# Projections of an attention layer: the two halves of each q, k and gate part in one PSUM bank, wide evacuations, and another split of the last scaling

## The chip, the core and the metric

The kernel runs on one core of a Trainium2 chip. The metric is the device time of one execution in microseconds (us). The engines are named as in the profile: PE is TensorE (PEld its weight loads), DVE is VectorE, ACT is ScalarE, POOL is GpSimd, SP is SyncE, whose queue issues nearly all DMAs.

## The reference

One layer of block attention on 256 positions of width 1024, 16 heads of 64, everything in float32:

```python
h = rms_norm(x, norm_g)
q, k, v, gate = jnp.split(h @ w_in, 4, axis=-1)     # w_in is 1024 x 4096
o = moba_attention(to_heads(q), to_heads(k), to_heads(v))
x = x + (o * jax.nn.silu(gate)) @ w_out             # w_out is 1024 x 1024
return rms_norm(x, final_norm_g)
```

With 256 positions there is a single block, so the attention is a plain causal softmax with a linear position penalty per head.

## The kernel before

*Precision.* A float32 matrix a is split into a rounded high part ah (written by ACT) and a remainder al = a - ah (written by DVE); a product is three matmuls, ah bh + al bh + ah bl. The input x times the norm's gain is held transposed as xh and xl, and each piece of weights w as whi and wlo, 128x1024 elements, one ACT and one DVE instruction per piece, from a piece that SP's queue fetched. The 1/rms of a position is not applied to x but to the results.

*Projections.* PARTS lists the order: v (first 512 columns), then q, k, g of 256 columns each, and so on, 14 parts. The first v part runs while the data arrive. A q, k or g part has 256 output columns, that is two pairs of heads, f = 0 and 1, of 128 rows each. Its loop (L661 to L684) takes two banks by take_now, one for each f, and runs over 8 slices of the depth, in each over f and the three terms, with 256 columns (positions) per matmul.

*Evacuation.* After the last matmul of each f, evac starts a fiber fiber_evac (L484 to L526): DVE multiplies the bank by rows (1/rms of each position, repeated in all partitions) or rows8 (the same over 8) into z, 128x256; ACT writes the high part of z as q or k (or tanh(z/2) for the gate, into sg, whose tile is called head in the profile), and DVE the remainder (L519) or (tanh + 1) z (L525). fiber_norm makes rows and rows8 on ACT (L650, L651). Since the gate is not halved, the softmax sums are doubled (L399) before the reciprocal.

*Attention.* scores(p) multiplies q and k of the two pairs p and p + 1 in four banks (L353, 16 or 20 matmuls shown per block); it waits for both pairs' q and k. Then each pair has its own fiber_pair: masks and minima on DVE (L386, L389), exponentials on ACT, scaling by the reciprocals (pr, L412), transposes on PE (L111), their split (pth on ACT, ptl on DVE), the product with v (matmuls pth, ptl with vv), the sum of its halves (cs on ACT, og on DVE, L467), the gate product (L471), and its split into oh (ACT) and ol (DVE, L476).

*What sets the order.* The program is written out by a planner at build time. Class Plan keeps one clock per engine, with costs per instruction. Fibers yield the time from which they want to go on; side, called after each matmul, advances the first fiber that is ready by that clock, and fill places the splits of the next weight piece when they become due. So a changed cost or a changed number of fibers moves instructions of other stages too. Each engine then runs its list in order and waits where an operand is not there. A tile pool with n buffers lets n tiles live at once; q had 4 tiles of one pair, k had 3.

*Output.* The output projection adds, for each of 8 pairs k, three matmuls per group of columns, with 512, 512 columns for the first 128 positions (block 0, m = 0) and 512, 256, 256 for the second (block 1, m = 1). Its tail (L712 to L749) adds x (L731), squares and sums on ACT (L737, the sum of a row comes by a separate accumulator read) or, for a block's last group, on DVE (L733), multiplies by the final gain (L738, L743), adds up the mean square (L739), takes the power -1/2 on POOL (L742), scales (ACT L744 for the first 512 columns, DVE L747 for the rest) and stores by SP's queue (L749). The scaled block lies in a tile that is called bias in the profile.

Of the kernel before, what the change touches and what calls it, by code (L numbers as in the profile page):

```python
# [13 lines left out]
P = 128  # L14
# [27 lines left out]
for seg in LAID:  # L42
# [2 lines left out]
        WIDTH[seg] = (NK if seg[1] == 0 else 0) + S * (seg[2] - seg[1])  # L45
    else:
        WIDTH[seg] = D if seg[0] == "t" else KP * GW // seg[3]
NKB = 3
NPR = 3
NPT = 3  # L50
SLACK = 1000.0
# [36 lines left out]
def trunk(ctx: ExitStack, tc, laid, fin_g, out):  # L88
# [6 lines left out]
    sm = ctx.enter_context(tc.tile_pool(name="sm", bufs=8))  # L95
    sp = ctx.enter_context(tc.tile_pool(name="sp", bufs=NPR))
    ptp = ctx.enter_context(tc.tile_pool(name="ptp", bufs=NPT))
    qp = ctx.enter_context(tc.tile_pool(name="qp", bufs=4))
    khp = ctx.enter_context(tc.tile_pool(name="khp", bufs=NKB))
    zp = ctx.enter_context(tc.tile_pool(name="zp", bufs=3))  # L100
    csp = ctx.enter_context(tc.tile_pool(name="csp", bufs=2))
    ogp = ctx.enter_context(tc.tile_pool(name="ogp", bufs=2))
    psum = ctx.enter_context(tc.tile_pool(name="psum", bufs=1, space=bass.MemoryType.PSUM))


    def mm(o, a, b, start, stop, n, dep=0.0):
        nc.tensor.matmul(o, a, b, start=start, stop=stop)  # L107
        return plan.mm(n, dep)

    def tr(o, a, dep=0.0):  # L110
# [103 lines left out]
    rstd = [const.tile([P, 1], F32, name=f"rstd{m}") for m in range(NM)]  # L214
    rows = const.tile([P, S], F32, name="rows")
    rows8 = const.tile([P, S], F32, name="rows8")

    def make_bias(h):
        slope = -(2.0 ** (-8.0 * (h + 1) / H))
# [104 lines left out]
    def scores(p):  # L324


        while not all(u in at_k and u in at_q for u in (p, p + 1)):
            yield poll()
        yield max(t[u] for t in (at_k, at_q) for u in (p, p + 1))
        while stage["s"] < p:  # L330
            yield poll()
        while True:
            b0 = take(keep[0] + 3)
            if b0 is not None:
                break
            yield poll()
        both = [b0] + [take_now() for _ in range(3)]
        plan.pe += SWITCH
        for u in (p, p + 1):
            of_pair[u] = both[2 * (u - p):2 * (u - p) + 2], {}  # L340
        for m, c in ((1, slice(0, S)), (0, slice(S, S + P))):
            for u in (p, p + 1):
                bs, at_s = of_pair[u]
                (qh, ql), kt = qs[u], ks[u]
# [12 lines left out]
        stage["s"] = p + 2  # L357
        yield 0

    def fiber_pair(p):  # L360
# [35 lines left out]
                    give(bs[a], d)  # L396
        stage["e"] += 1
        yield e - 400
        nc.vector.tensor_scalar(rs, rs, 2.0, None, op0=ALU.mult)  # L399
        dve(4, e)  # L400
        yield plan.t["dve"] - 50
        nc.vector.reciprocal(ri, rs)
        d = d_ri = dve(4, e, extra=157)
        for a in range(2):
# [74 lines left out]
    def evac(kind, j, f, b, r):  # L479
        fibers.insert(0, [0.0, fiber_evac(kind, j, f, b, r)])  # L480
        if kind == "k":
            fibers.append([0.0, fiber_pair(2 * j + f)])

    def fiber_evac(kind, j, f, b, r):  # L484
        ps = b["t"][:, :S]
        p = 2 * j + f
        if kind == "v":
            ps = b["t"]
# [13 lines left out]
        while not have_rows:  # L502
            yield poll()
        yield max(r, have_rows[0]) - 200
        z = zp.tile([P, S], F32, name="z")
        nc.vector.tensor_mul(z, ps, rows8 if kind == "q" else rows)  # L506
        d = dve(S, max(r, have_rows[0]))
        give(b, d)
        if kind == "k":
            while stage["s"] <= p - NKB:  # L510
                yield poll()
        yield d - 100
        if kind != "g":
            pool = qp if kind == "q" else khp
            both = pool.tile([P, 2, S], F32R, name=kind)
            hi, lo = both[:, 0], both[:, 1]
            e = act(hi, z, AF.Copy, S, d, False)
            yield e - 100
            nc.vector.tensor_sub(lo, z, f32(hi))  # L519
            (qs if kind == "q" else ks)[p] = (hi, lo) if kind == "q" else both  # L520
            (at_q if kind == "q" else at_k)[p] = dve(S, e)
        else:
            e = act(sg[:, p, :], z, AF.Tanh, S, d, False, scale=0.5)
            yield e - 100
            nc.vector.scalar_tensor_tensor(sg[:, p, :], sg[:, p, :], 1.0, z, op0=ALU.add, op1=ALU.mult)  # L525
            at_g[p] = dve(S, e)  # L526

    with tc.manual_schedule():

# [96 lines left out]
        def fiber_norm():  # L626
# [22 lines left out]
            yield r - 200  # L649
            act(rows, b["t"][:, :S], AF.Copy, S, r, True)  # L650
            d = act(rows8, b["t"][:, :S], AF.Copy, S, r, True, scale=DH ** -0.5)  # L651
            give(b, d)
            have_rows.append(d)
# [5 lines left out]

        i = 3  # L660
        for kind, j in PARTS[1:]:  # L661
            acc = [take_now() for _ in range(2)]
            dep = [b["free"] for b in acc]
            w = CW if kind == "v" else GW
            kp = KP * GW // w
            for k in range(NK):
# [5 lines left out]
                for f in range(2):  # L672
                    fs = slice(f * P, (f + 1) * P)
                    for jj, (xx, ww) in enumerate(((xh, whi), (xl, whi), (xh, wlo))):
                        if kind == "v":
                            o, a, b = acc[f]["t"], xx[k][:, fs], ww[i][:, kk * w:(kk + 1) * w]
                        else:
                            o, a, b = acc[f]["t"][:, :S], ww[i][:, kk * w + f * P:kk * w + (f + 1) * P], xx[k]
                        r = mm(o, a, b, k == 0 and jj == 0, k == NK - 1 and jj == 2, w if kind == "v" else S,
                               max(wr, dep[f]))  # L680
                        fill()
                        side()
                    if k == NK - 1:
                        evac(kind, j, f, acc[f], r)  # L684


# [16 lines left out]
        for k in range(NK):  # L703
            use(N_IN + k - (k >= 5))
            if k < NK - 4:
                until(lambda: k in at_o)
                plan.pe = max(plan.pe, at_o[k])
                for m in range(NM):
                    for c0, c1 in GROUPS[m]:
                        outmm(k, m, c0, c1, accs[m, c0]["t"][:, :c1 - c0])  # L710
        use(N_PIECES)
        for m in range(NM):  # L712
            y, z, sq = xs[m], spare[:, m * D:(m + 1) * D], spare[:, 2 * D + m * CW:2 * D + (m + 1) * CW]
            ns = len(GROUPS[m])
# [9 lines left out]
            for u, (c0, c1) in enumerate(GROUPS[m]):  # L724
                c = slice(c0, c1)
                o = accs[m, c0]["t"][:, :c1 - c0]
                for k in range(late, NK):
                    until(lambda: k in at_o)
                    plan.pe = max(plan.pe, at_o[k])
                    outmm(k, m, c0, c1, o)  # L730
                nc.vector.tensor_add(y[:, c], o, y[:, c])  # L731
                if u == ns - 1:
                    nc.vector.tensor_tensor_reduce(sq[:, :c1 - c0], y[:, c], y[:, c], scale=1.0 / D,  # L733
                                                   scalar=ms[:, u - 1:u], op0=ALU.mult, op1=ALU.add,
                                                   accum_out=ms[:, u:u + 1])
# [53 lines left out]
```

## Time and profile before

| | |
|---|---|
| three runs | 145.71, 146.01, 146.97 us, median 146.01 |
| profiled execution | 146.19 us, its span in the trace 144.4 us |
| PE busy | 136.7 us (95%), weight loads 125.9 us |
| DVE busy | 123.0 us (85%) |
| ACT busy | 93.3 us (65%) |
| POOL busy | 13.7 us (10%) |
| TensorE clock granted | 0.993 of full speed over the span |

The span reaches from the first to the last instruction; the rest of the execution's own time lies around it. Busy times of different engines overlap. A matmul's busy time is modelled and longer than the distance to the next start, since matmuls are pipelined. In rows with a time in front, the first number is the start in us from the span's start, the second the duration, and what stands in brackets is idle time of that engine just before and what ended it.

### The profile page before, as it was taken

The page shows a single profiled execution, that of the slowest core. Times are in us where ns is not written, and L with a number is a line of the kernel's source. Part 1 is how long each engine was busy: PE and PEld are TensorE (multiplying, and loading weights), DVE is VectorE, ACT ScalarE, POOL GpSimd, SP SyncE. Part 2 cuts the span into 40 slices and gives each one's busy share as a digit, 9 for nine tenths or more (in the row PEclk, how much of TensorE's full clock was granted, in tenths as well). Part 3 has the DMA queues.
Part 4 walks back from the last instruction along what each step waited for, and adds up shares of the span by engine and source line. Part 5 has one row for each costly group of instructions (what it writes and reads, how often), then busy time and mean ns, then how long its engine had stood idle before and what let it go on. Part 6 is the DMA issues. An engine that isn't in the chain of part 4 may idle for free.

```text
span 144.4 us, 2750 instructions
## 1 busy us (share of the span) xinstructions
PE 136.7 (95%) x993; PEld 125.9 (87%) x993; DVE 123.0 (85%) x306; ACT 93.3 (65%) x198; POOL 13.7 (10%) x29
## 2 busy tenths in 40 slices
PE   7999999999999999999999999999999999999910
PEld 5678899999999999999987899999999889887900
DVE  0999489979988899989999998978989989965870
ACT  3498979665789572979855798536394884622331
POOL 7892140000000000000000000000000000000210
PEclk9999999999999999999999999999999999999997
DMA  5999998588005275622456601567756040000123
GB/s 167 327 394 413 408 390 301 204 284 292 31 0 183 112 242 178 211 100 86 174 176 199 235 9 32 178 210 231 246 168 222 33 138 9 0 0 0 41 109 145
DMA packets 8078, 24.83 MB, mean 172 GB/s; under 512 B 896, under 2 KB 1408, under 8 KB 8064
## 3 DMA queue, kind: packets, MB, share of 16 engines
q1 hardware_dynamic: 7632, 23.73, 47.5%
q10 hardware_dynamic: 432, 0.92, 1.7%
q8 instruction: 8, 0.13, 0.4%
q14 instruction: 6, 0.05, 0.1%
HBM read 23.60 MB, written 1.05 MB: 171 GB/s over the span
## 4 chain that ended last, share of the span: by engine, by line
PE 77%; DMA 8%; DVE 4%; issue 4%; ACT 2%; SPq 1%; POOL 1%; POOLq 0%; ACTq 0%
PE bank L107 70%; DMA w<-in_laid 8%; PE bank L111 4%; PE bank L353 4%; DVE wlo L251 2%; ACT whi L118 1%; DVE x L731 1%; SPq L157 1%; POOL fr L742 1%; DVE bias L733 1%; ACT bias L737 1%; ACT bias L744 0%; POOLq L785 0%; DVE xl L572 0%; ACT head L118 0%
## 5 line engine op out<-in xcount | busy, mean ns | idle before, releaser
L107 PE MATMUL bank<-xh,wlo 128*128 128x256 f32 x192 | 55.3, 288 | 0.0
L107 PE MATMUL bank<-xh,whi 128*128 128x256 f32 x192 | 55.1, 287 | 0.0
L107 PE MATMUL bank<-xl,whi 128*128 128x256 f32 x192 | 55.1, 287 | 0.0
L118 ACT ACTIVATE whi<-w 128x1024 fp32r<-128x1024 f32 (+1 forms) x43 | 42.0, 977 | 17.8 <-PE bank L107 10.4
L251 DVE TENSOR_TENSOR wlo<-w,whi 128x1024 fp32r<-128x1024 f32 (+1 forms) x43 | 48.6, 1139 | 4.6 <-ACT whi L118 4.5
L107 PEld LDWEIGHTS bank<-xh,wlo 128*128 128x128 f32 x192 | 36.2, 189 | 0.3 <-DVE wlo L251 0.2
L107 PEld LDWEIGHTS bank<-xh,whi 128*128 128x128 f32 x192 | 36.2, 189 | 0.2
L107 PEld LDWEIGHTS bank<-xl,whi 128*128 128x128 f32 x192 | 36.3, 189 | 0.1
L118 ACT ACTIVATE pr<-st,mx 128x256 f32<-128x256 f32 (+1 forms) x32 | 14.2, 443 | 3.8 <-DVE mx L389 3.8
L742 POOL TENSOR_TENSOR fr<-fms,mhalf 128x1 f32<-128x1 f32 x2 | 1.6, 799 | 117.4 <-DVE fms L733 117.4
L107 PE MATMUL bank<-whi,oh 128*128 128x512 f32 (+1 forms) x35 | 12.7, 363 | 0.0
L107 PE MATMUL bank<-whi,ol 128*128 128x512 f32 (+1 forms) x35 | 12.7, 363 | 0.0
L107 PE MATMUL bank<-wlo,oh 128*128 128x512 f32 (+1 forms) x35 | 12.6, 360 | 0.0
L107 PE MATMUL bank<-whi,xh 128*128 128x512 f32 x32 | 12.3, 426 | 0.0
L111 PE MATMUL bank<-ident,pr 128*128 128x128 f32 x48 | 12.0, 272 | 0.0
L107 PE MATMUL bank<-whi,xl 128*128 128x512 f32 x32 | 11.8, 409 | 0.0
L107 PE MATMUL bank<-wlo,xh 128*128 128x512 f32 x32 | 11.4, 398 | 0.0
L506 DVE TENSOR_TENSOR z<-bank,rows 128x256 f32<-128x256 f32 x24 | 9.2, 419 | 1.5 <-PE bank L107 1.3
L435 DVE TENSOR_TENSOR ptl<-bank,pth 128x384 fp32r<-128x384 f32 x16 | 8.8, 554 | 1.4 <-ACT pth L118 1.1
L118 ACT ACTIVATE pth<-bank 128x384 fp32r<-128x384 f32 x16 | 7.9, 491 | 3.0 <-PE bank L111 2.7
L107 PE MATMUL bank<-ptl,vv 128*128 128x256 f32 (+1 forms) x32 | 8.9, 278 | 0.0
L220 POOL TENSOR_SCALAR bias<-dist 128x256 f32<-128x256 f32 x16 | 8.7, 544 | 1.0
(79 smaller groups left out, 204.4 us busy)
## 6 DMA issues: line engine op xcount, KB each, us to landing
w<-in_laid SPq DMA_DIRECT2D x36, 512.0 KB, 4.1
w<-in_laid SPq DMA_DIRECT2D x7, 256.0 KB, 5.4
x<-in_laid SPq DMA_DIRECT2D x2, 512.0 KB, 6.9
head<-in_laid SPq DMA_DIRECT2D x3, 256.0 KB, 5.6
out<-bias SPq DMA_DIRECT2D x2, 320.0 KB, 2.3
gf<-in_fin_g ACTq DMA_DIRECT2D x1, 512.0 KB, 5.5
out<-bias SPq DMA_DIRECT2D x2, 192.0 KB, 1.9
w<-in_laid ACTq DMA_DIRECT2D x1, 256.0 KB, 3.0
```

Of the source, the lines that this page charges most:

```text
L107: nc.tensor.matmul(o, a, b, start=start, stop=stop)
L111: nc.tensor.transpose(o, a, ident)
L118: nc.scalar.activation(o, i, fn, scale=scale, **kw)
L157: (queue or nc.sync).dma_start(o, laid[START[seg]:START[seg] + n].rearrange("(p n) -> p n", p=P))
L220: nc.gpsimd.tensor_scalar(bias[:, h, :], dist, slope, 0.0, op0=ALU.mult, op1=ALU.add)
L251: nc.vector.tensor_sub(wlo[i][:, c], w32[i][:, c], f32(whi[i][:, c]))
L353: nc.tensor.matmul(o, q[rr, m * P:(m + 1) * P], kt[rr, ts[0]:ts[-1] + 1, 0:n], start=jj == 0, stop=jj == len(terms) - 1, skip_group_check= ...
L435: nc.vector.tensor_sub(lo[:, a], pv, f32(hi[:, a]))
L506: nc.vector.tensor_mul(z, ps, rows8 if kind == "q" else rows)
L731: nc.vector.tensor_add(y[:, c], o, y[:, c])
L733: nc.vector.tensor_tensor_reduce(sq[:, :c1 - c0], y[:, c], y[:, c], scale=1.0 / D, scalar=ms[:, u - 1:u], op0=ALU.mult, op1=ALU.add, accum ...
L742: nc.gpsimd.tensor_tensor(r, ms[:, ns - 1:ns], mhalf, op=ALU.pow)
```

## The change

A q, k or g part now takes one bank; f = 0 goes to its first 256 columns and f = 1 to the last, in the same order of matmuls, and only the very first matmul of the bank has the start flag. One fiber_evac per part works on 128x512: one z product, one high part, one remainder. The tiles of q and k hold two pairs, with 2 buffers each, z has 2. The gate's z is made with rowsh, which holds 1/rms over 2 and is one more ACT instruction of 128x256 in fiber_norm; so ACT's tanh needs no factor, and the doubling of the softmax sums is gone. A score block's fiber, and those of its two pairs, are started when the part's evacuation starts. In the tail, block 0's scaling is done by ACT alone, in two instructions of 512 columns: one as soon as the power is there, the other after the square of block 1's first group; each is followed by a store of its 512 columns. The additions of the mean square (add_square) are written after the next group's add, except for the last group of block 1, where it stands ahead of it.

```diff
-NKB = 3
+NKB = 2
...
-    qp = ctx.enter_context(tc.tile_pool(name="qp", bufs=4))
+    qp = ctx.enter_context(tc.tile_pool(name="qp", bufs=NKB))
     khp = ctx.enter_context(tc.tile_pool(name="khp", bufs=NKB))
-    zp = ctx.enter_context(tc.tile_pool(name="zp", bufs=3))
+    zp = ctx.enter_context(tc.tile_pool(name="zp", bufs=2))
...
-        nc.vector.tensor_scalar(rs, rs, 2.0, None, op0=ALU.mult)
-        dve(4, e)
-        yield plan.t["dve"] - 50
         nc.vector.reciprocal(ri, rs)
...
-        z = zp.tile([P, S], F32, name="z")
-        nc.vector.tensor_mul(z, ps, rows8 if kind == "q" else rows)
-        d = dve(S, max(r, have_rows[0]))
+        pairs = slice(2 * j, 2 * j + 2)
+        ps = ps.rearrange("p (f n) -> p f n", f=2)
+        z = zp.tile([P, 2, S], F32, name="z")
+        rb = {"q": rows8, "k": rows, "g": rowsh}[kind].unsqueeze(1).to_broadcast([P, 2, S])
+        nc.vector.tensor_mul(z, ps, rb)
+        d = dve(2 * S, max(r, have_rows[0]))
         give(b, d)
-        if kind == "k":
-            while stage["s"] <= p - NKB:
+        if kind != "g":
+            while stage["s"] < 2 * (j - NKB + 1):
                 yield poll()
         yield d - 100
         if kind != "g":
             pool = qp if kind == "q" else khp
-            both = pool.tile([P, 2, S], F32R, name=kind)
-            hi, lo = both[:, 0], both[:, 1]
-            e = act(hi, z, AF.Copy, S, d, False)
+            both = pool.tile([P, 2, 2, S], F32R, name=kind)
+            e = act(both[:, 0], z, AF.Copy, 2 * S, d, False)
             yield e - 100
-            nc.vector.tensor_sub(lo, z, f32(hi))
+            nc.vector.tensor_sub(both[:, 1], z, f32(both[:, 0]))
...
         else:
-            e = act(sg[:, p, :], z, AF.Tanh, S, d, False, scale=0.5)
+            e = act(sg[:, pairs, :], z, AF.Tanh, 2 * S, d, False)
             yield e - 100
-            nc.vector.scalar_tensor_tensor(sg[:, p, :], sg[:, p, :], 1.0, z, op0=ALU.add, op1=ALU.mult)
+            nc.vector.scalar_tensor_tensor(sg[:, pairs, :], sg[:, pairs, :], 1.0, z, op0=ALU.add, op1=ALU.mult)
...
+            d = act(rowsh, b["t"][:, :S], AF.Copy, S, r, True, scale=0.5)
...
-            acc = [take_now() for _ in range(2)]
+            acc = [take_now() for _ in range(2 if kind == "v" else 1)] * (1 if kind == "v" else 2)
...
-                            o, a, b = acc[f]["t"][:, :S], ww[i][:, kk * w + f * P:kk * w + (f + 1) * P], xx[k]
+                            o, a, b = acc[f]["t"][:, f * S:(f + 1) * S], ww[i][:, kk * w + f * P:kk * w + (f + 1) * P], xx[k]
...
-                    if k == NK - 1:
+                    if k == NK - 1 and (kind == "v" or f == 1):
                         evac(kind, j, f, acc[f], r)
...
+        later = []
+
+        def scale_first(z, r, c0, c1):
+            nc.scalar.activation(z[:, c0:c1], z[:, c0:c1], AF.Copy, scale=r)
+            nc.sync.dma_start(out[0, 0:P, c0:c1], z[:, c0:c1])
+
+        def add_square(ms, ss, u):
+            nc.vector.scalar_tensor_tensor(ms[:, u:u + 1], ss[:, u:u + 1], 1.0 / D,
+                                           eps_t if u == 0 else ms[:, u - 1:u], op0=ALU.mult, op1=ALU.add)
...
+                if u == ns - 1 and m > 0:
+                    add_square(ms, ss, u - 1)
                 nc.vector.tensor_add(y[:, c], o, y[:, c])
+                if 0 < u < ns - 1 or m == 0 and u > 0:
+                    add_square(ms, ss, u - 1)
...
-                    nc.vector.scalar_tensor_tensor(ms[:, u:u + 1], ss[:, u:u + 1], 1.0 / D,
-                                                   eps_t if u == 0 else ms[:, u - 1:u], op0=ALU.mult, op1=ALU.add)
+                    for f in later:
+                        f()
+                    later = []
...
+            if m == 0:
+
+                scale_first(z, r, 0, CW)
+                later.append(lambda z=z, r=r: scale_first(z, r, CW, D))
+                continue
```

Two places show how the lists move. The first is the tail on DVE, before: x_102 is block 0 and x_103 block 1, and L747 is block 0's scaling.

```order
L743 TENSOR_TENSOR bias<-x_102,gf 128x512
L747 TENSOR_SCALAR bias<-bias,fr 128x384
L747 TENSOR_SCALAR bias<-bias,fr 128x128
L731 TENSOR_TENSOR x_103<-bank_95,x_103 128x512
L738 TENSOR_TENSOR bias<-x_103,gf 128x512
L739 SCALAR_TENSOR_TENSOR fms<-fss,eps_t 128x1
L731 TENSOR_TENSOR x_103<-bank_94,x_103 128x256
L738 TENSOR_TENSOR bias<-x_103,gf 128x256
L739 SCALAR_TENSOR_TENSOR fms<-fss,fms 128x1
L731 TENSOR_TENSOR x_103<-bank_99,x_103 128x256
```

The same stretch of DVE's list now (L748 is the add, L724 add_square):

```order
L763 TENSOR_TENSOR bias<-x_102,gf 128x512
L748 TENSOR_TENSOR x_103<-bank_96,x_103 128x512
L757 TENSOR_TENSOR bias<-x_103,gf 128x512
L748 TENSOR_TENSOR x_103<-bank_99,x_103 128x256
L724 SCALAR_TENSOR_TENSOR fms<-fss,eps_t 128x1
L757 TENSOR_TENSOR bias<-x_103,gf 128x256
L724 SCALAR_TENSOR_TENSOR fms<-fss,fms 128x1
L748 TENSOR_TENSOR x_103<-bank_95,x_103 128x256
```

And ACT's tail before, where L744 scales and L737 squares:

```order
L737 ACTIVATE bias,fss<-x_102 128x512
L744 ACTIVATE bias<-bias,fr 128x512
L737 ACTIVATE bias,fss<-x_103 128x512
L737 ACTIVATE bias,fss<-x_103 128x256
L744 ACTIVATE bias<-bias,fr 128x512
```

and now (L756 squares, L720 is scale_first, L769 the scaling of block 1):

```order
L756 ACTIVATE bias,fss<-x_102 128x512
L720 ACTIVATE bias<-bias,fr 128x512
L756 ACTIVATE bias,fss<-x_103 128x512
L720 ACTIVATE bias<-bias,fr 128x512
L756 ACTIVATE bias,fss<-x_103 128x256
L769 ACTIVATE bias<-bias,fr 128x512
```

DVE lost its two scalings of block 0, and ACT has one more, between the two squares of block 1.

The second place is DVE ahead of the third block of scores (pairs 4 and 5), from the first cs sum of the two pairs before to the last k remainder (L519). Before:

```order
L467 TENSOR_TENSOR og<-bank_96,cs 64x256 x2
L435 TENSOR_TENSOR ptl<-bank_98,pth 128x384
L519 TENSOR_TENSOR k<-z,k 128x256
L471 TENSOR_TENSOR og<-og,head 128x256
```

and now:

```order
L465 TENSOR_TENSOR og<-bank_100,cs 64x256 x2
L252 TENSOR_TENSOR wlo<-w_804,whi 128x1024
L469 TENSOR_TENSOR og<-og,head 128x256
L507 TENSOR_TENSOR z<-bank_98,rows 128x512
L465 TENSOR_TENSOR og<-bank_95,cs 64x256 x2
L474 TENSOR_TENSOR ol<-og,oh 128x256
L469 TENSOR_TENSOR og<-og,head 128x256
L519 TENSOR_TENSOR k<-z,k 128x512
```

Both pairs' sums and gate products and one ol now stand ahead of the k remainder; before, k was split with one pair's sums ahead. On PE the same block of scores had 30 matmuls of v's second part (128x512) ahead of it and now has 15; the second block has 12 matmuls of 128x256 fewer ahead of it, the fourth 6 more.

## Rows read from the trace of the kernel before

**Rows 1.** The page: busy shares, PE and DVE by slices, the chain by engine.

```profile
PE 136.7 (95%) x993; PEld 125.9 (87%) x993; DVE 123.0 (85%) x306; ACT 93.3 (65%) x198; POOL 13.7 (10%) x29
...
PE   7999999999999999999999999999999999999910
...
DVE  0999489979988899989999998978989989965870
...
PE 77%; DMA 8%; DVE 4%; issue 4%; ACT 2%; SPq 1%; POOL 1%; POOLq 0%; ACTq 0%
```

**Rows 2.** Waits of PE's weight loads: total us, times, longest.

```profile
PEld bank L107 <- ACT whi L118: 1.0, 2, 0.7
PEld bank L353 <- issue: 0.4, 1, 0.4
PEld bank L107 <- DVE wlo L251: 0.2, 1, 0.2
```

**Rows 3.** Timeline of PE: first and last of ten and of twelve matmuls.

```profile
76.39 0.39 PE L107 MATMUL bank<-wlo,xh 128*128 128x512 f32 x1
...
78.49 0.39 PE L107 MATMUL bank<-wlo,xh 128*128 128x512 f32 x1
...
98.50 0.28 PE L107 MATMUL bank<-xh,whi 128*128 128x256 f32 x1
...
99.79 0.28 PE L107 MATMUL bank<-xh,wlo 128*128 128x256 f32 x1
```

**Rows 4.** Groups by line and form on DVE: busy us, mean ns, idle before.

```profile
L506 DVE TENSOR_TENSOR z<-bank,rows 128x256 f32<-128x256 f32 x24 | 9.2, 419 | 1.5 <-PE bank L107 1.3
...
L731 DVE TENSOR_TENSOR x<-bank,x 128x512 f32<-128x512 f32 x3 | 2.1, 686 | 2.1 <-PE bank L107 2.1
...
L399 DVE TENSOR_SCALAR rs<-rs 128x4 f32<-128x4 f32 x8 | 1.2, 165 | 0.2
```

**Rows 5.** Timeline of DVE: the first two z products, merged.

```profile
24.15 0.75 DVE L506 TENSOR_TENSOR z<-bank,rows 128x256 f32<-128x256 f32 x2
```

**Rows 6.** Timeline of the tail, all engines.

```profile
134.37 0.69 DVE L743 TENSOR_TENSOR bias<-x,gf 128x512 f32<-128x512 f32 x1
...
134.49 0.39 PE L107 MATMUL bank<-xh,ol 128*128 128x512 f32 x1
...
135.50 0.73 ACT L744 ACTIVATE bias<-bias,fr 128x512 f32<-128x512 f32 x1 [2.63 <-POOL fr L742]
135.50 0.62 DVE L747 TENSOR_SCALAR bias<-bias,fr 128x384 f32<-128x384 f32 x2 [0.44 <-POOL fr L742]
...
136.03 0.68 DVE L731 TENSOR_TENSOR x<-bank,x 128x512 f32<-128x512 f32 x1
...
136.75 0.63 ACT L737 ACTIVATE bias<-x 128x512 f32<-128x512 f32 x1 [0.52 <-DVE x L731]
...
137.29 0.19 ACT L737 ACTIVATION_READ_ACCUMULATOR bias<-x 128x1 f32 x1
...
137.46 0.28 PE L107 MATMUL bank<-xh,ol 128*128 128x256 f32 x1
...
138.10 0.42 ACT L737 ACTIVATE bias<-x 128x256 f32<-128x256 f32 x1 [0.62 <-DVE x L731]
138.42 0.19 ACT L737 ACTIVATION_READ_ACCUMULATOR bias<-x 128x1 f32 x1
138.64 0.16 DVE L739 SCALAR_TENSOR_TENSOR fms<-fss,fms 128x1 f32<-128x1 f32 x1 [0.18 <-ACT bias L737]
138.71 0.42 DVE L731 TENSOR_TENSOR x<-bank,x 128x256 f32<-128x256 f32 x1
```

**Rows 7.** Timeline: k's last remainder and the scores, third and fourth block.

```profile
73.83 0.41 DVE L519 TENSOR_TENSOR k<-z,k 128x256 fp32r<-128x256 f32 x1
...
78.81 1.39 PE L353 MATMUL bank<-k,q 64*128 64x256 f32 x20
...
98.77 0.76 DVE L519 TENSOR_TENSOR k<-z,k 128x256 fp32r<-128x256 f32 x2
...
100.00 1.33 PE L353 MATMUL bank<-k,q 64*128 64x256 f32 x18
```

More of the change, by code (lines that the diff above doesn't have):

```diff
@@ L106, in mm @@
     def mm(o, a, b, start, stop, n, dep=0.0):
-        nc.tensor.matmul(o, a, b, start=start, stop=stop)
+        nc.tensor.matmul(o, a, b, start=start, stop=stop, skip_group_check=True)
         return plan.mm(n, dep)
@@ L216, in trunk @@
     rows8 = const.tile([P, S], F32, name="rows8")
+    rowsh = const.tile([P, S], F32, name="rowsh")
     def make_bias(h):
@@ L343, in scores @@
                 bs, at_s = of_pair[u]
-                (qh, ql), kt = qs[u], ks[u]
+                (qh, ql), kt = (qs[u][:, 0], qs[u][:, 1]), ks[u]
                 n = c.stop - c.start
@@ L481, in evac @@
         if kind == "k":
-            fibers.append([0.0, fiber_pair(2 * j + f)])
+            for a in range(2):
+                fibers.append([0.0, fiber_pair(2 * j + a)])
     def fiber_evac(kind, j, f, b, r):
-        ps = b["t"][:, :S]
-        p = 2 * j + f
+        ps = b["t"]
         if kind == "v":
-            ps = b["t"]
             hs = slice(j * H // 2, (j + 1) * H // 2)
@@ L514, in fiber_evac @@
             pool = qp if kind == "q" else khp
-            both = pool.tile([P, 2, S], F32R, name=kind)
-            hi, lo = both[:, 0], both[:, 1]
-            e = act(hi, z, AF.Copy, S, d, False)
+            both = pool.tile([P, 2, 2, S], F32R, name=kind)
+            e = act(both[:, 0], z, AF.Copy, 2 * S, d, False)
             yield e - 100
-            nc.vector.tensor_sub(lo, z, f32(hi))
-            (qs if kind == "q" else ks)[p] = (hi, lo) if kind == "q" else both
-            (at_q if kind == "q" else at_k)[p] = dve(S, e)
+            nc.vector.tensor_sub(both[:, 1], z, f32(both[:, 0]))
+            d = dve(2 * S, e)
+            for a in range(2):
+                (qs if kind == "q" else ks)[2 * j + a] = both[:, :, a]
+                (at_q if kind == "q" else at_k)[2 * j + a] = d
         else:
-            e = act(sg[:, p, :], z, AF.Tanh, S, d, False, scale=0.5)
+            e = act(sg[:, pairs, :], z, AF.Tanh, 2 * S, d, False)
             yield e - 100
-            nc.vector.scalar_tensor_tensor(sg[:, p, :], sg[:, p, :], 1.0, z, op0=ALU.add, op1=ALU.mult)
-            at_g[p] = dve(S, e)
+            nc.vector.scalar_tensor_tensor(sg[:, pairs, :], sg[:, pairs, :], 1.0, z, op0=ALU.add, op1=ALU.mult)
+            d = dve(2 * S, e)
+            at_g[2 * j] = at_g[2 * j + 1] = d
     with tc.manual_schedule():
@@ L651, in fiber_norm @@
             d = act(rows8, b["t"][:, :S], AF.Copy, S, r, True, scale=DH ** -0.5)
+            have_rows.append(d)
+            d = act(rowsh, b["t"][:, :S], AF.Copy, S, r, True, scale=0.5)
             give(b, d)
-            have_rows.append(d)
         fibers.append([x_at[0], fiber_norm()])
@@ L677, in trunk @@
                         else:
-                            o, a, b = acc[f]["t"][:, :S], ww[i][:, kk * w + f * P:kk * w + (f + 1) * P], xx[k]
-                        r = mm(o, a, b, k == 0 and jj == 0, k == NK - 1 and jj == 2, w if kind == "v" else S,
-                               max(wr, dep[f]))
+                            o, a, b = acc[f]["t"][:, f * S:(f + 1) * S], ww[i][:, kk * w + f * P:kk * w + (f + 1) * P], xx[k]
+                        r = mm(o, a, b, k == 0 and jj == 0 and (kind == "v" or f == 0), k == NK - 1 and jj == 2,
+                               w if kind == "v" else S, max(wr, dep[f]))
                         fill()
                         side()
-                    if k == NK - 1:
+                    if k == NK - 1 and (kind == "v" or f == 1):
                         evac(kind, j, f, acc[f], r)
```

## The prediction

> **What bounds the kernel now.** I read the page's busy shares first, then the chain, then TensorE's waits, then the spacing of matmuls, and only then the tail. TensorE (PE) is busy in nearly every slice from the second to the 38th, and the chain that ends last lies on it for 77% of the span [rows 1]. A busy PE is a modelled figure, since matmuls overlap, so the spacing of starts is the better test. The waits of PE's weight loads are the check from the other side: before 21 us two on ScalarE's whi (1.0 us) and one on VectorE's wlo (0.2 us); after it one of 0.4 us, ahead of the last block of scores [rows 2]. Eleven spacings of 256-column matmuls take 99.79 - 98.50 = 1.29 us, 0.117 each, and nine of 512 columns 78.49 - 76.39 = 2.10 us, 0.233 each [rows 3]. So from 21 us until PE ends at 137.5 us nothing that VectorE (DVE) or ScalarE (ACT) does holds PE up, although DVE is 85% busy. A gain can come from the 0.4 us, from the early waits, or from the tail behind PE; a loss from any wait that the new order puts on PE.
>
> **The change, part by part.**
>
> *Matmuls.* Their number, shapes and start order within a part stay; a pair's halves now share a bank instead of having one each. No row shows two interleaved halves. Nearest rows: consecutive matmuls into one bank and into another bank stand at the same 0.117 us [rows 3], so I take 0. A price per half switch is the unknown: 12 parts x 16 groups of three = 192 switches; the one dear step in these rows, from the projections to the scores, takes 100.00 - 99.79 = 0.21 instead of 0.117, 0.09 more [rows 3, 7]. The bounds are 0 and 192 x 0.09 = 17 us. A half switch is nearer to a bank switch, where kind and operands stay and only the destination changes, than to that step, so I stay at 0.
>
> *Evacuations.* 12 z products, 8 q/k remainders and 4 gate products lose one instruction each, 24 pairs of 256 columns becoming 24 of 512. By means a pair saves 2 x 0.419 - 0.686 = 0.15 us, 24 x 0.15 = 3.6 us of DVE; eight doublings of the softmax sums (L399) go too, 8 x 0.165 = 1.3 us [rows 4]. Where DVE has no gap, two 256-column products take 0.75 us together [rows 5], so a wide one saves only 0.75 - 0.69 = 0.06 us, 1.4 us over all. On ACT 12 pairs become 12 wide copies or tanh, and one more row copy comes, both hidden. DVE saves 1.4 to 4.9 us, ACT about 2 at most, and since PE waits for neither, I cost all of this at 0 on the path. The cover is PE's own queue of projections; without it each late piece costs its lateness.
>
> The Trainium skill, page "VectorE: DVE Perf Modes", section on the TRN2 errata, says that each SBUF-source operation pays a fixed latency between instructions and advises tiles of 512 elements or more. By it the saving would be the full fixed part of 24 instructions, the 3.6 us above; the dense pair of rows 5 shows 0.06 us each, so here the measurement takes most of it back.
>
> *The new order.* The third block of scores moves most: 15 matmuls of 512 columns stand before it in v's second part, where there were 30. It starts at 78.81 - 15 x 0.233 = 75.3 us [rows 3, 7]. Its last operand, the k remainder, ended at 73.83 + 0.41 = 74.24 [rows 7]. In the new queue the other pair's two cs sums (2 x 0.41, a 64-partition form at about the price of a 256-column product), its gate product and its ol remainder (0.42 each, same price [rows 4]) come ahead of it, +1.7 us, while one wlo of 128x1024 leaves; twice the 512-column price less one overlap, some 1.2 us, is my estimate for that. k is then ready at about 74.7, 0.6 us ahead. The fourth block starts 6 x 0.117 = 0.7 us later, at 100.7; k's remainder has one more wlo ahead and ends at 98.77 + 0.76 + 0.7 = 100.2, 0.5 us ahead, the margin it had [rows 7]. I take no new wait: 0, with 0 to 0.6 us as the soft end.
>
> *The tail.* In block 0 the sum add_square (0.16 us) now stands between the add and the square-reduce that needs both; before, it waited in front of the add for ACT [rows 6]. I take 0, either way at most 0.1. The two DVE scalings (L747, 0.62 us from 135.50) leave. They kept block 1's first add until 136.03, though its bank's last matmul had started at 134.49 and lasted 0.39, until 134.88, and the DVE product before ended at 134.37 + 0.69 = 135.06 [rows 6]. So the add starts at 135.08, 0.95 earlier, and ends at 135.8. ACT is now the path. It starts block 0's scaling at 135.50 as before (0.73 us). A following ACT operation starts 0.09 us before the end of the one in front: the square at 136.75 lasts 0.63, its accumulator read starts at 137.29 [rows 6]. So:
> - the square of block 1's first part: 135.50 + 0.64 = 136.14, before 136.75; its read starts at 136.68 and ends at 136.87
> - block 0's second scaling, new here, 0.73 us: 136.78 to 137.51
> - the square of the second part: 137.42, before 138.10; its read ends 0.51 later, 137.93, before 138.42 + 0.19 = 138.61
> - the sum follows at 137.96 and the last add 0.07 later at 138.03, before 138.71 [rows 6].
>
> PE's last bank is complete at 137.46 + 0.28 = 137.74 and does not bind. The rest (reduce, power, scaling, store) keeps its length. The gain is 138.71 - 138.03 = 0.68 us. Without any overlap on ACT the square would start at 136.23, the second scaling at 136.96, the second square at 137.69, the add at 138.30: 0.41. I take 0.6, since the row shows the overlap. The four stores become 2 x 256 KB and the two of block 1; block 0's second one is issued at 137.5 instead of about 136.3, over 3 us ahead of the last two, so it costs nothing.
>
> **Sum.** The profiled execution took 146.19 us (span 144.4, 1.8 outside), 0.18 over the median of 146.01. 146.19 - 0.6 = 145.59 on it, 146.01 - 0.6 = 145.4 on the median.
>
> **The rivals.**
> - *Part of the gain is eaten.* The tail gives only 0.41, or a score block waits some tenths for its k. For it: both margins are estimates of 0.5 and 0.6 us. Against: the planner places a block behind its operands, and the margins measured before (0.5 us at the fourth) held. Time: 145.6 (tail only) to 146.2 (0.41 less 0.6 of waits).
> - *Slower: k is late for the moved score block.* One chain, z, copy, remainder for both pairs, now hangs on one DVE queue, and PE, in order, stands still at the third block with v's projections queued behind it. It costs its lateness one to one from 75.3 us on. For a loss of 1%, k must end at 75.3 + 0.6 + 1.5 = 77.4 or later, 3.2 us after it ended before. DVE has 9 tenths in those slices [rows 1], so nothing is made up; against it, DVE has less work in all. Time with 2.5 us of waits: 146.01 - 0.6 + 2.5 = 147.9.
> - *Slower: half switches cost.* From 2.1/192 = 0.011 us a switch on it loses 1%. 0.02 each gives 145.4 + 3.8 = 149.2. Nothing shows it.
> - *Faster: DVE was the second bound.* If all of the 4.9 us came back, 145.4 - 4.9 = 140.5. By the errata rule cited above this would be the main effect of wider tiles. Against it: after 21 us PE waits 0.4 us in all [rows 2], and the early waits are for weight pieces that are split in the same order as before, so at most 0.4 us can come back, to 145.0.
> - *The wide operations are no faster than the pairs*, because the row operand is repeated by a zero stride. Then DVE saves nothing; PE still hides it. Same time as the forecast.
>
> **How the numbers follow.** Two kernels less than 1% (1.5 us) apart can't be told apart here, once and for all. Forecast (144.9 to 145.6, with the 0.4 us perhaps returned): 0.54. Part eaten: 0.29. Slower by k: 0.09, by switches 0.02. Faster by over 1% (below 144.55): 0.06, all from the DVE rival. The likeliest time is 145.4. The range from 144.8 to 146.7 takes in the two middle cases, 0.83, with a little for the spread of the three runs (145.71 to 146.97), and leaves out the outer ones. Faster 0.06, same 0.83, slower 0.11.
>
> **What would show it.** In the changed kernel's profile: spacings of 0.117 us in the q, k and g parts (otherwise the half switches); no PE or weight-load wait at about 75 and 101 us, or its length (k late); block 1's first add at about 135.1, the two new ACT scalings some 1.3 us apart, the last add about 0.6 us earlier against PE's end (the tail); DVE's busy time down by 1 to 5 us with PE's end in place (cover). The forecast is wrong if PE ends more than 1 us earlier or later, or if ACT's order delays the last square beyond 138.1 counted from the old start.

## The result, and the profile after

The changed kernel takes 145.19 us (median of 14 runs, 144.92 to 146.48); the kernel before, timed in turn with it, 146.17 us (14 runs, 145.70 to 147.35). The ratio is 0.9934, interval 0.9906 to 0.9961: a gain of 0.98 us. The interval leaves out 1, and the gain is below the 1% that the forecast set as its bound of no change. The profiled execution took 145.19 us with a span of 143.0, against 146.19 and 144.4.

The page of the change (busy shares, the slices of PE), which answers to [rows 1]:

```profile
PE 136.0 (95%) x993; PEld 124.9 (87%) x993; DVE 119.6 (84%) x270; ACT 93.2 (65%) x190; POOL 13.6 (10%) x29
...
PE   7999999999999999999999999999999999999930
```

DVE has 36 instructions and 3.4 us less to do, inside the 1.4 to 4.9 us of the forecast, and PE is as full as it was. The groups by line and form on DVE, the answer to [rows 4], show where it went: the 24 narrow products are 12 wide ones of 0.69 us.

```profile
L507 DVE TENSOR_TENSOR z<-bank,rows 128x512 f32<-128x512 f32 x8 | 5.5, 686 | 0.9 <-PE bank L107 0.9
L507 DVE TENSOR_TENSOR z<-bank,rowsh 128x512 f32<-128x512 f32 x4 | 2.8, 690 | 0.6 <-PE bank L107 0.6
```

PE did not get this time. Besides the wait at the program's start (1.0 us, in both kernels) and two of 0.2 us before 21 us, its weight loads wait for these (total us, times, longest), the answer to [rows 2]:

```profile
PEld bank L107 <- ACT whi L118: 0.8, 1, 0.8
PEld bank L107 <- DVE wlo L252: 0.7, 2, 0.5
PEld bank L354 <- issue: 0.4, 1, 0.4
```

The 0.4 us is still there. It stands ahead of the third block of scores, at 74.97 now and at 78.81 before, and not ahead of the last block, as the forecast says. It is also idle time of the weight loads and not of PE: PE's own step to that block was 78.81 - 78.49 = 0.32 us before [rows 3, 7], 0.09 more than a step between two projections. So about 0.1 us could have come back there, not 0.4.

The timeline of PE in a part whose two halves share a bank, the answer to [rows 3], has 14 spacings in 98.70 - 97.06 = 1.64 us, 0.117 each, half switches included:

```profile
97.06 0.28 PE L107 MATMUL bank<-xh,whi 128*128 128x256 f32 x1
...
98.70 0.28 PE L107 MATMUL bank<-xh,wlo 128*128 128x256 f32 x1
```

The timeline of k's remainders and of the third and fourth block of scores, the answer to [rows 7]: k ends at 74.48 and the block starts at 74.97; k ends at 99.77 and the block starts at 100.32.

```profile
73.80 0.68 DVE L519 TENSOR_TENSOR k<-z,k 128x512 fp32r<-128x512 f32 x1
74.97 1.39 PE L354 MATMUL bank<-k,q 64*128 64x256 f32 x20
...
99.08 0.69 DVE L519 TENSOR_TENSOR k<-z,k 128x512 fp32r<-128x512 f32 x1
100.32 0.86 PE L354 MATMUL bank<-k,q 64*128 64x256 f32 x10
```

The tail is where something moved. Its timeline in the change (start, duration, engine, line), the answer to [rows 6], from the product ahead of block 0's second add on:

```profile
131.68 0.69 DVE L757 TENSOR_TENSOR bias<-x,gf 128x512 f32<-128x512 f32 x1
...
132.29 0.68 DVE L748 TENSOR_TENSOR x<-bank,x 128x512 f32<-128x512 f32 x1
132.89 0.15 DVE L724 SCALAR_TENSOR_TENSOR fms<-fss,eps_t 128x1 f32<-128x1 f32 x1
133.07 0.75 DVE L752 CUSTOM_DVE_ANT_0 bias<-x,fms 128x512 f32<-128x512 f32 x1
...
134.88 0.73 ACT L720 ACTIVATE bias<-bias,fr 128x512 f32<-128x512 f32 x1 [2.48 <-POOL fr L762]
...
135.88 0.42 DVE L748 TENSOR_TENSOR x<-bank,x 128x256 f32<-128x256 f32 x1
...
136.12 0.71 ACT L720 ACTIVATE bias<-bias,fr 128x512 f32<-128x512 f32 x1
...
136.74 0.40 ACT L756 ACTIVATE bias<-x 128x256 f32<-128x256 f32 x1
...
136.99 0.28 PE L107 MATMUL bank<-xh,ol 128*128 128x256 f32 x1
137.04 0.19 ACT L756 ACTIVATION_READ_ACCUMULATOR bias<-x 128x1 f32 x1
...
137.26 0.16 DVE L724 SCALAR_TENSOR_TENSOR fms<-fss,fms 128x1 f32<-128x1 f32 x1 [0.50 <-ACT bias L756]
137.34 0.42 DVE L748 TENSOR_TENSOR x<-bank,x 128x256 f32<-128x256 f32 x1
```

The number to carry through what follows is the distance from the start of PE's last matmul to the start of the last add, since a shift of the whole program drops out of it. It is 137.34 - 136.99 = 0.35 us here and was 138.71 - 137.46 = 1.25 [rows 6]. So the tail gained 0.90 us by the trace. The rest of the difference between the two profiles, 0.47 us at PE's last matmul, is half there (0.24) at the first matmul of the first q part, which starts at 16.23 instead of 16.47, ahead of the first wide evacuation; the last section returns to that.

### The profile page after: what moved, and what is told of

The parts are those of the page before. It is cut to its first block, busy times and chain, and to the rows that moved or that the text cites. A ratio compares the mean times of both kernels' runs of the same rounds, so it can differ in the third digit from the quotient of the medians.

```text
span 143.0 us, 2690 instructions
## 1 busy us (share of the span) xinstructions
PE 136.0 (95%) x993; PEld 124.9 (87%) x993; DVE 119.6 (84%) x270; ACT 93.2 (65%) x190; POOL 13.6 (10%) x29
## 4 chain that ended last, share of the span: by engine, by line
PE 86%; DMA 3%; issue 3%; DVE 3%; POOL 1%; SPq 1%; ACT 1%; POOLq 0%; DVEq 0%
PE bank L107 79%; PE bank L111 4%; PE bank L354 4%; DMA head<-in_laid 3%; DVE x L748 1%; POOL fr L762 1%; DVE wlo L252 1%; SPq L157 1%; DVE bias L752 1%; ACT bias L769 1%; POOLq L810 0%; DVE bias L757 0%; DVE fms L724 0%; DVEq L575 0%; DVE fms L752 0%
## 5 line engine op out<-in xcount | busy, mean ns | idle before, releaser
L111 PE MATMUL bank<-ident,pr 128*128 128x128 f32 x48 | 11.8, 272 | 0.0
L107 PE MATMUL bank<-whi,xh 128*128 128x512 f32 x32 | 11.6, 404 | 0.1
L107 PE MATMUL bank<-pth,vv 128*128 128x256 f32 (+1 forms) x32 | 8.0, 251 | 0.0
```

The costliest lines, as they stand in the source:

```text
L107: nc.tensor.matmul(o, a, b, start=start, stop=stop, skip_group_check=True)
L111: nc.tensor.transpose(o, a, ident)
```

## The experiments

Two readings were set against each other. T: all of the gain is made in the tail, and the wider evacuations are hidden. D: the evacuations matter, because DVE is close to being a second bound. In all diffs a minus is the kernel that the run starts from.

**1. Only the tail.** The kernel before, with narrow evacuations, gets the tail of the change.

```diff
...
+                if u == ns - 1 and m > 0:
+                    add_square(ms, ss, u - 1)
                 nc.vector.tensor_add(y[:, c], o, y[:, c])
+                if 0 < u < ns - 1 or m == 0 and u > 0:
+                    add_square(ms, ss, u - 1)
...
+            if m == 0:
+                scale_first(z, r, 0, CW)
+                later.append(lambda z=z, r=r: scale_first(z, r, CW, D))
+                continue
```

> The kernel before with the changed tail alone; the evacuations are the old pairs of 256 columns. Theory T (the whole gain lies in the tail): last add of block 1 starts 0.35 us after PE's last matmul starts (before 1.25, change 0.35), time 0.9 us under before, ratio 0.994. Rival D (a part comes from VectorE's shorter evacuations, since PE's last matmul started 0.47 us earlier in the trace of the change): same tail, but only about 0.5 us under before, ratio 0.9965.

Measured: 145.02 us, ratio 0.9937 (0.9913 to 0.9960). In its timeline the last matmul and the last add stand 0.34 us apart:

```profile
137.38 0.28 PE L107 MATMUL bank<-xh,ol 128*128 128x256 f32 x1
...
137.72 0.42 DVE L743 TENSOR_TENSOR x<-bank,x 128x256 f32<-128x256 f32 x1
```

**2. Only the evacuations.** The change, with the tail of the kernel before.

```diff
...
-                if u == ns - 1 and m > 0:
-                    add_square(ms, ss, u - 1)
                 nc.vector.tensor_add(y[:, c], o, y[:, c])
-                if 0 < u < ns - 1 or m == 0 and u > 0:
-                    add_square(ms, ss, u - 1)
...
+                    nc.vector.scalar_tensor_tensor(ms[:, u:u + 1], ss[:, u:u + 1], 1.0 / D,
+                                                   eps_t if u == 0 else ms[:, u - 1:u], op0=ALU.mult, op1=ALU.add)
...
-                scale_first(z, r, 0, CW)
-                later.append(lambda z=z, r=r: scale_first(z, r, CW, D))
-                continue
```

> The change with the old tail; the evacuations are 512 wide. T: last add 1.25 us after PE's last matmul starts, as before; ratio 1.000, within 0.3 us; PE's start at the first q part may differ by 0.2 us from run to run, as that comes ahead of every changed instruction. D: ratio 0.9965, PE's last matmul 0.4 to 0.5 us earlier than before.

Measured: 146.13 us, ratio 1.0006 (0.9978 to 1.0034), with DVE's busy time down to 120.4 us from 123.0. The distance in the tail is the old one, 1.26 us. The page's first line, and the timeline:

```profile
PE 136.4 (95%) x993; PEld 125.9 (87%) x993; DVE 120.4 (83%) x272; ACT 92.8 (64%) x189; POOL 13.6 (9%) x29
...
137.29 0.28 PE L107 MATMUL bank<-xh,ol 128*128 128x256 f32 x1
...
138.55 0.42 DVE L736 TENSOR_TENSOR x<-bank,x 128x256 f32<-128x256 f32 x1
```

Runs 1 and 2 split the change in two, and the split is clean: the tail alone gives all of the gain, the evacuations alone nothing. D's 0.9965 lies outside both intervals. T holds and D falls.

**3. Only the place of the sums.** That left a size to explain: the trace's 0.90 us is more than the 0.68 that the ACT chain should give. This is the kernel before with the sum (add_square) written behind the next add, and nothing else.

```diff
...
+                if u == ns - 1 and m > 0:
+                    add_square(ms, ss, u - 1)
                 nc.vector.tensor_add(y[:, c], o, y[:, c])
+                if 0 < u < ns - 1 or m == 0 and u > 0:
+                    add_square(ms, ss, u - 1)
...
-                    nc.vector.scalar_tensor_tensor(ms[:, u:u + 1], ss[:, u:u + 1], 1.0 / D,
-                                                   eps_t if u == 0 else ms[:, u - 1:u], op0=ALU.mult, op1=ALU.add)
```

> The kernel before, with only the additions of the mean square written after the next group's add; block 0's scaling stays half on VectorE. Own step as predicted (this reordering is worth 0): last add 1.25 us after PE's last matmul, ratio 1.000. New reading of the change's trace (it lets the adds of both blocks start before ScalarE's sums are there): block 0's square-reduce 0.15 us earlier, block 1's second add no longer behind the sum, last add 0.85 us after PE's last matmul, 0.4 us gained, ratio 0.997.

Measured: 145.64 us, ratio 0.9992 (0.9970 to 1.0014). In the timeline the distance is 0.88 us instead of 1.25, a gain of 0.37:

```profile
137.02 0.28 PE L107 MATMUL bank<-xh,ol 128*128 128x256 f32 x1
...
137.90 0.42 DVE L737 TENSOR_TENSOR x<-bank,x 128x256 f32<-128x256 f32 x1
```

The times don't confirm that. A gain of 0.37 us would be a ratio of 0.9975, inside the interval but near its edge; no change is inside as well. The trace of one execution shows the mechanism, the timing can't tell its size from nothing.

**4. Only the scaling.** The kernel before with block 0's scaling on ACT, the sums where they were.

```diff
...
-                    nc.vector.scalar_tensor_tensor(ms[:, u:u + 1], ss[:, u:u + 1], 1.0 / D,
-                                                   eps_t if u == 0 else ms[:, u - 1:u], op0=ALU.mult, op1=ALU.add)
+                    add_square(ms, ss, u)
+                    for f in later:
+                        f()
+                    later = []
...
+            if m == 0:
+                scale_first(z, r, 0, CW)
+                later.append(lambda z=z, r=r: scale_first(z, r, CW, D))
+                continue
```

> The kernel before, with only block 0's scaling moved to ScalarE in two instructions with a store each; the sums stay ahead of the adds. As predicted: block 1's first add about 0.95 us earlier, last add 0.57 us after PE's last matmul starts (0.68 gained), ratio 0.9953. If ScalarE's operations did not overlap: 0.84 us after, 0.41 gained, ratio 0.997.

Measured: 145.45 us, ratio 0.9967 (0.9949 to 0.9986). The interval takes in both expected ratios, so the timeline has to decide. It has 138.20 - 137.58 = 0.62 us, a gain of 0.63:

```profile
135.63 0.72 ACT L715 ACTIVATE bias<-bias,fr 128x512 f32<-128x512 f32 x1 [2.64 <-POOL fr L754]
...
136.26 0.62 ACT L747 ACTIVATE bias<-x 128x512 f32<-128x512 f32 x1
...
136.87 0.71 ACT L715 ACTIVATE bias<-bias,fr 128x512 f32<-128x512 f32 x1
...
137.07 0.42 DVE L741 TENSOR_TENSOR x<-bank,x 128x256 f32<-128x256 f32 x1
...
137.58 0.28 PE L107 MATMUL bank<-xh,ol 128*128 128x256 f32 x1
137.59 0.42 ACT L747 ACTIVATE bias<-x 128x256 f32<-128x256 f32 x1
...
138.20 0.42 DVE L741 TENSOR_TENSOR x<-bank,x 128x256 f32<-128x256 f32 x1
```

ACT starts the three at 135.63, 136.26 and 136.87, 0.63 and 0.61 us apart where the forecast had 0.64: the overlap is as it had assumed. Block 1's first add starts at 135.10, ahead of the first scaling, so DVE no longer holds that square. The second square starts 0.72 us behind the scaling in front of it instead of 0.64, since block 1's second add ends only at 137.07 + 0.42 = 137.49. So the 0.68 us of the scaling was right to 0.05. With the sums as well, run 1, the gain is 0.91: the place of the sums adds 0.28 on top.

**5. The halves switch at every matmul.** In the change a half gets three matmuls in a row; here the two halves of the bank take turns, six switches in each slice of the depth where there were two.

```diff
-                for f in range(2):
+                terms = ((xh, whi), (xl, whi), (xh, wlo))
+                todo = [(f, jj) for f in range(2) for jj in range(3)] if kind == "v" else \
+                    [(f, jj) for jj in range(3) for f in range(2)]
+                for f, jj in todo:
...
```

> The change, with the two halves of a bank alternating at every matmul of a q, k or g part (terms outside, halves inside), 48 matmuls per depth group of 8 slices, so 48 - 1 half switches per part where there were 16. T (a half switch is free): spacing 0.117 us as before, ratio 0.9934 as for the change, within 0.3%. Rival (a switch costs c): 12 x 32 = 384 more switches, so 0.005 us a switch would already show as 1.9 us, ratio above 1.005.

Measured: 145.17 us, ratio 0.9934 (0.9910 to 0.9957), the same as the change. In its timeline of PE the pairs (one matmul into each half, merged into a row of two) start 25.86 - 23.75 = 2.11 us apart over nine steps, 0.117 a matmul:

```profile
23.75 0.40 PE L107 MATMUL bank<-xh,whi 128*128 128x256 f32 x2
...
25.86 0.40 PE L107 MATMUL bank<-xh,whi 128*128 128x256 f32 x2
```

A half switch costs nothing that this can show.

**6. Each wide product twice.** To see how deep the cover is, DVE makes each of the 12 z products two times.

```diff
         nc.vector.tensor_mul(z, ps, rb)
+        nc.vector.tensor_mul(z, ps, rb)
```

> The change, with each of the 12 wide z products done twice into the same tile: 12 x 0.6 to 0.69 = 7.2 to 8.3 us more VectorE work, twice what the wide form saved at most, in the same order of instructions. T (VectorE is covered by PE's queue except right before a score block): PE waits only ahead of the score blocks, 0 to 0.8 us each, 0.5 to 2.5 us in all, ratio 0.997 to 1.010. Rival D (VectorE is a second bound): 7 us or more, ratio about 1.04.

Measured: 148.37 us, ratio 1.0150 (1.0114 to 1.0186). DVE is busy for 127.1 us, 7.5 more than in the change; PE's last matmul starts at 140.50, 3.51 later, and the time is 3.2 us longer. The waits of PE's weight loads that are new:

```profile
PEld bank L354 <- DVE k L520: 1.9, 3, 0.7
...
PEld bank L107 <- DVE ptl L433: 0.7, 2, 0.5
...
PEld bank L111 <- ACT pr L118: 0.4, 1, 0.4
...
PEld bank L111 <- ACT whi L118: 0.4, 1, 0.4
```

Neither reading had this: more than the 0.5 to 2.5 us of T, less than half of what D asked for. About half of the added work comes out on PE, three times ahead of a block of scores and four times ahead of the transposes (L111) and the products with v. The cover is real but not deep: taking 2.6 us off DVE (run 2) bought nothing, putting 7.5 on cost 3.2.

**7. One k remainder late.** The third block's k remainder is done four times, and with it the chain of the slower rival is made to happen.

```diff
-            nc.vector.tensor_sub(both[:, 1], z, f32(both[:, 0]))
+            for _ in range(4 if (kind, j) == ("k", 2) else 1):
+                nc.vector.tensor_sub(both[:, 1], z, f32(both[:, 0]))
```

> The change, with the third block's k remainder done four times into the same tile: about 3 x 0.63 = 1.9 us more on VectorE ahead of the third score block. In the change k ended 0.5 us before that block. T (k's lateness past that margin is paid one to one): PE stands still about 1.4 us ahead of the third block, ratio 0.9934 + 1.4/146 = 1.003. Rival (the lateness is given back by PE later, or the margin is larger): ratio stays within 0.9934 +- 0.002.

Measured: 146.85 us, ratio 1.0047 (1.0026 to 1.0068), 1.66 us over the change. Its timelines of PE and of DVE at the third block:

```profile
74.90 0.39 PE L354 MATMUL bank<-k,q 64*128 64x256 f32 x2
76.65 0.62 PE L354 MATMUL bank<-k,q 64*128 64x256 f32 x6 [1.36 <-DVE k L520]
...
73.73 2.87 DVE L520 TENSOR_TENSOR k<-z,k 128x512 fp32r<-128x512 f32 x4
```

The remainders end at 76.60 and the third matmul of the block starts at 76.65; two spacings behind 74.90 it would have started at about 75.1. That is some 1.6 us of lateness, and the kernel pays 1.66. So the rival's rule, one to one, holds in this run; what didn't come true in the change is its condition. The rows also say what the remainder is late for: the first two matmuls of the block run without it, so in the change the margin is a little more than the 75.0 - 74.5 = 0.5 us to the block's start.

**8. The last two stores from two queues.** The rest of the tail, from the last add to the end of the span, is 143.0 - 137.34 = 5.66 us in the change. This run sends block 1's halves from ACT's queue and from SP's.

```diff
+            nc.vector.tensor_scalar(z[:, CW:D], z[:, CW:D], r, None, op0=ALU.mult)
+            nc.sync.dma_start(out[0, m * P:(m + 1) * P, CW:D], z[:, CW:D])
             nc.scalar.activation(z[:, 0:CW], z[:, 0:CW], AF.Copy, scale=r)
-            cut = D - GW - P
-            for c0, c1 in ((cut, D), (CW, cut)):
-                nc.vector.tensor_scalar(z[:, c0:c1], z[:, c0:c1], r, None, op0=ALU.mult)
-            for c0, c1 in ((cut, D), (0, cut)):
-                nc.sync.dma_start(out[0, m * P:(m + 1) * P, c0:c1], z[:, c0:c1])
+            nc.scalar.dma_start(out[0, m * P:(m + 1) * P, 0:CW], z[:, 0:CW])
```

> The change, with block 1's last scaling as one 512-column half on each of VectorE and ScalarE, stored as 256 KB each from SP's queue and from ScalarE's own queue, instead of 192 and 320 KB both from SP. T (the span ends with the last store's landing, 2.3 us for 320 KB and 2.0 for 256 KB in the change's trace, and the second issue on SP stands behind the first): span ends 0.3 to 0.5 us earlier after PE's last matmul, ratio 0.9905 to 0.992. Rival (the two stores share the same transfer engines and end together): ratio 0.993.

Measured: 145.53 us, ratio 0.9961 (0.9943 to 0.9980), and 143.5 - 137.69 = 5.81 us behind the last add, about 0.15 more (spans are read to 0.1 us). The expected gain didn't come: both expected ratios lie below the interval. The issues by line (queue, count, KB, us from issue to landing) show where it went:

```profile
out<-bias SPq DMA_DIRECT2D x3, 256.0 KB, 2.0
...
out<-bias ACTq DMA_DIRECT2D x1, 256.0 KB, 2.5
```

The store is issued right behind ACT's scaling, 140.16 - 139.41 = 0.75 us after the scaling's start and some 0.1 us sooner than in the change (139.9 - 139.06), but takes 2.5 us to land; in the change the larger one of 320 KB from SP's queue takes 2.3. What was saved in the issue was lost in the landing. The two stores were under way at the same time, SP's from 139.93 on, so this run doesn't tell a slower queue from a shared transfer. The kernel's whole time is 0.34 us above the change's, and the profiles put as much ahead of PE's last matmul (137.33 against 136.99), where the two kernels don't differ: not all of it is the stores' doing. No version beats the change.

## Why the prediction was right, and where it was short

**What bounds the kernel.** Right. PE's spacing has no room in it, and run 2 shows that a faster DVE is worth nothing (1.0006). The rival that DVE was the second bound fell with it, as far as less work on DVE goes; more work does reach PE (run 6). The reading of PE's waits against DVE's 85% busy was what decided this.

**Matmuls.** 0 was taken between 0 and 17 us; run 5 has the switches three times as frequent at the same time. The upper end, taken from a step between two kinds of matmuls, was no price of a half switch.

**Evacuations.** Hidden, as costed. The saving of DVE, 3.4 us, lies inside the stated 1.4 to 4.9, but these ends were not added up alike. The lower one leaves out the eight doublings, 1.3 us by the forecast's own price, and both leave out block 0's two scalings, 0.6 us, which the change takes off DVE as well. With them the 0.06 us a pair of [rows 5] gives 1.4 + 1.3 + 0.6 = 3.3 us, and the means 5.5. Run 2, without the new tail, has 123.0 - 120.4 = 2.6 us. Of these 1.2 are the doublings by their busy time in [rows 4], and two scalings of pr that now run on ACT are in it too (27 on DVE before, 25 in run 2), which leaves some 1.4 us at most for the 24 pairs. That is the price of [rows 5], taken where DVE has no gap, and not the 0.15 us a pair of the means. The forecast named PE's queue as the cover and didn't size it. Run 6 does, from the other side only.

**The new order.** k was to be ready at 74.7 and 100.2 for blocks at 75.3 and 100.7. The rows have 74.48 and 99.77 for 74.97 and 100.32, all 0.2 to 0.4 us earlier, as all of the program was from the first q part on; the margins of 0.5 to 0.6 us came out at 0.49 and 0.55. No wait, and run 7 shows what one would have cost.

**The tail, the step that was short.** The place and the mechanism were right, the chain on ACT to 0.05 us (run 4). The failed step is the sentence on the sum: "I take 0, either way at most 0.1". In the kernel before the sum stands ahead of block 0's second add and holds it until ACT has squared the first group. The timeline of DVE before has it:

```profile
132.14 0.69 DVE L738 TENSOR_TENSOR bias<-x,gf 128x512 f32<-128x512 f32 x1
132.90 0.16 DVE L739 SCALAR_TENSOR_TENSOR fms<-fss,eps_t 128x1 f32<-128x1 f32 x1
132.98 0.68 DVE L731 TENSOR_TENSOR x<-bank,x 128x512 f32<-128x512 f32 x1
133.70 0.75 DVE L733 CUSTOM_DVE_ANT_0 bias<-x,fms 128x512 f32<-128x512 f32 x1
```

From the product's start to the add's it is 0.84 us before and 132.29 - 131.68 = 0.61 in the change. The sum now runs between the add and the square-reduce and takes part of that back, so the square-reduce starts 1.39 us behind the product instead of 1.56: 0.17 earlier, and with it the power and the first scaling. That scaling starts 2.11 us ahead of PE's last matmul in the change, 1.96 before. Run 3, which moves nothing but the sums, has 1.40 and 2.11. The forecast had set the sum's two places against each other as equal; but in the old place it cost its wait for ACT as well, in the new place only its 0.15 us. Block 1's second add moves in the same way: it starts at 135.88 and ends at 136.30, before ACT asks for it at 136.74, while in run 4 it ends at 137.49, with the sum's wait for ACT ahead of it, and holds the second square. The chain on ACT from the first scaling to the last add is thereby 137.34 - 134.88 = 2.46 us where run 4 has 138.20 - 135.63 = 2.57. So run 4's 0.63 us became 0.90. The forecast had worked out 0.68 and took 0.6; by the traces the tail was 0.30 us short, 0.22 of it against the 0.68. That 145.4 still lies only 0.2 us above the measured 145.19 is in part luck: the forecast started from the median of three runs, 146.01, and the kernel before took 146.17 when it was timed with the change, so the gain by the times was 0.98 us where 0.6 was forecast. That the 0.27 us over run 4 is the sums is the traces' word (runs 1, 3 and 4); the times of runs 1 and 4, 0.9937 and 0.9967, point the same way with intervals that overlap.

The end of this gain is in sight, too. PE's last bank is complete at 136.99 + 0.28 = 137.27 and ACT's last read ends at 137.23, with the last add at 137.34. By these rows, in which a matmul's end is modelled, more speed on ACT or DVE could move that add by at most 0.07 us.

## What to carry to other kernels

Where one engine's starts stand at a constant spacing to within a few tenths of the end, work taken off the others is worth what lies behind the last of those starts, here a microsecond, whatever the busy shares say; but the cover has a depth, and taking work away measures nothing of it, only adding some does. Price a merged instruction from rows where its engine has no gap: here a pair saved some 0.06 us, and the means of single durations promised 0.15. When a small instruction that waits for another engine changes its place in an in-order queue, cost the wait in front of everything queued behind it, not the instruction's own duration. And measure a tail as a distance between two of its own instructions: between two executions the whole program shifted by more than one term of the sum.

## What the runs showed of the hardware that was not expected

The program's first matmuls run slower in some of the ten profiles, one of each kernel, and for a different time in each. The timeline of PE in the kernel before has two 512-column matmuls from 4.40 to 5.42, 0.51 us each:

```profile
4.40 1.22 PE L107 MATMUL bank<-whi,xh 128*128 128x512 f32 x2
5.42 0.89 PE L107 MATMUL bank<-whi,xl 128*128 128x512 f32 x2
```

The change's has the same two from 4.51 to 5.08, 0.28 each:

```profile
4.51 0.73 PE L107 MATMUL bank<-whi,xh 128*128 128x512 f32 x2
5.08 0.63 PE L107 MATMUL bank<-whi,xl 128*128 128x512 f32 x2
```

Later such a matmul starts every 0.233 us. The first matmul of the first q part then starts at 16.23 to 16.25 us in the change and in runs 3, 5, 6 and 7, at 16.47 in the kernel before, at 16.67 to 16.82 in runs 1, 2, 4 and 8. The groups don't follow the edits: run 8's kernel differs from the change's only behind the last add, and yet has 16.70 where the change has 16.23. From there to the last matmul the kernel before takes 120.99 us and the change 120.76, runs 1 to 4 120.59 to 120.77. So up to 0.6 us between two single profiles need not come from an edit. What it depends on stays open. The windows of the trace give a granted clock of 1.00, the level of 2.4 GHz, for 4 to 10 us in the kernel before and in the change alike, with the seven matmuls on oh (L535 before, L538 now, from 1.0 us) in front of them in both. The Trainium skill, page "TensorE: Matmul & The Clock Gate", section "What's actually happening", says that the engine begins at its lower clock level and that the number of matmuls that run so differs between runs of the same kernel. The varying start agrees with that; the recorded clock doesn't, and no run here decides between them.

A store of 256 KB landed 2.5 us after its issue from ACT's queue and 2.0 us from SP's (run 8, one store against the median of three). ACT's went out while one of SP's was still under way, so the queue itself isn't shown to be slower.
